# A two-layer attention and convolution trunk: the softmax's division moved into the output gate

## The chip, the cores and the metric

The kernel runs on one core of one Trainium2 chip. The metric is the device time of one execution in microseconds; the time before is the median of three runs, 1473.94 us (1473.72 to 1475.07). The profiled execution is a further one. The core's engines are TensorE (PE, with its weight loads as PEld), VectorE (DVE), ScalarE (ACT), GpSimd (POOL) and SyncE (SP), which issues the DMAs here.

## What is computed

The input x has 256 tokens of 2048 channels, in float32. Two layers follow each other. The first is attention with three groups of 16 heads (windows and dilations 128/1, 512/4, 2048/16), whose three outputs are merged for each head slot by their softmax denominators, and multiplied by a SiLU gate z:

```
proj = rmsnorm(x) @ w_in                       # q, k, v of 3 groups x 16 heads x 128, and z
o_g, lse_g = attention of group g (QK-norm, bias, window)
w = softmax over the groups of lse_g
y = (sum over g of w_g * o_g) * silu(z)        # silu(z) = z * sigmoid(z)
x = x + y @ w_out
```

Merging three softmaxes by their denominators is the same as one softmax over the keys of all three groups, and so the kernel computes it: one set of scores of 512 columns per head and block of 128 tokens. The second layer is a convolution module with gated projections; the change does not touch it.

## The kernel before

All large products are made in three matmuls of rounded parts: an operand is split in a high part `hi` and the remainder `lo`, and hi x hi, lo x hi and hi x lo are summed. `stage` (lines 101 to 111) loads one chunk of weights (128 x 1024), casts it to `hi` on ScalarE (line 109) and subtracts it to `lo` on VectorE or GpSimd (line 110), three chunks ahead of its use. `low_engine` chooses: VectorE for almost all chunks of the input projection, GpSimd for the chunks 3 to 15 of the output projection's 32.

The order of all work is written out by hand. The main loop has one step per chunk, n. A step stages chunk n + 3, issues the matmuls of chunk n, and then runs the functions that `at(n, ...)` entered in a table for this step, in the order in which they were entered. Each engine executes its own instructions in the order of issue. The input projection has 320 chunks: 8 head sets of 40, two heads each; a chunk is 12 matmuls of 512 columns (lines 257 to 259). A chunk of the output projection is 24 matmuls of 256 columns (lines 493 to 496).

While the projection of the next set runs, the heads of one set are worked off in four units (head h and token block b, in the order h0 b0, h0 b1, h1 b0, h1 b1), three steps apart; in the last set, which runs beside the output projection, two steps apart. A unit, whose first step is t, goes through:
- t: `scores` on TensorE (lines 344 to 356);
- t + 1: `softmax` (358 to 371): bias added and the row maximum taken on VectorE, then exp with the row sum on ScalarE (line 371);
- t + 2: `weigh` (373 to 377): the reciprocal of the sum on VectorE (line 375), and the 512 exponentials multiplied by it on GpSimd (line 377);
- t + 3: `turn` (379 to 382): four transpositions on TensorE into a PSUM tile `pt`;
- t + 4: `split` (384 to 391): `pt` into high and low part, on ScalarE and VectorE.

After the second unit of a head come `values` (t + 5, lines 393 to 412), the matmuls with v; `gated` (t + 6, 414 to 420), which adds the two halves of their result and multiplies with the gate; and `y_split` (t + 7).

The gate: `z_take` copies z out of PSUM, scaled by the token's norm factor r0; `z_gate` (333 to 339), once for each token block, computes z / (1 + exp(-z)) with an exp on ScalarE and an addition, a reciprocal and a product on VectorE; `z_turn` (431 to 436) transposes the four 128 x 128 blocks of a set in one step, e + 4, where e is the set's last projection step, into one PSUM tile; `z_put` (438 to 440) copies it to SBUF one step later.

PSUM tiles come from rings. The ring `t` has two buffers, which `turn`, the scores of groups 1 and 2 (`sy`), the transpositions of q and k (`psq`) and `z_turn` use in turn; a new tile waits until the one before the last has been read. In the last set `z_turn` takes the ring `o` of the value matmuls.

Of the kernel before, what the change touches and what calls it, by code (L numbers as in the profile page):

```python
# [11 lines left out]
F32 = mybir.dt.float32  # L12
F32R = mybir.dt.float32r
AF = mybir.ActivationFunctionType
ALU = mybir.AluOpType
AX = mybir.AxisListType

P = 128
# [7 lines left out]
NSET = 8  # L26
# [15 lines left out]
def hybrid_kernel(ctx: ExitStack, tc: tile.TileContext, x_perm, x_nat, vecs, rel, onehot, maskrow,  # L42
                  w_in, w_out, v_in, v_out, out):
    nc = tc.nc
    cpool = ctx.enter_context(tc.tile_pool(name="cpool", bufs=1))
# [6 lines left out]
    def bank(tag, name, bufs):  # L52
        return psum.tile([P, 512], F32, tag=tag, name=name, bufs=bufs)
# [4 lines left out]
    def t_tile(name):  # L58
        return bank("t", name, 2)
# [10 lines left out]
    def at(n, fn, *args):  # L70
        steps.setdefault(n, []).append((fn, args))
# [43 lines left out]
    ident = cpool.tile([P, P], F32, name="ident")  # L115
# [5 lines left out]
    def rsqrt_mean(dst, src, count, n):  # L121

        nc.gpsimd.tensor_scalar(dst, src, 1.0 / count, EPS, op0=ALU.mult, op1=ALU.add)  # L123
        nc.gpsimd.tensor_tensor(dst, dst, nhalf[:, :n], op=ALU.pow)  # L124
# [8 lines left out]
    apool = ph1.enter_context(tc.tile_pool(name="apool", bufs=1))  # L133

    r0 = cpool.tile([P, 2], F32, name="r0")
    nr0 = cpool.tile([P, 2], F32, name="nr0")
    gqk = cpool.tile([P, NG], F32, name="gqk")
    ssx = apool.tile([P, S], F32, name="ssx")

# [33 lines left out]
    def token_sums(ps, c0, src):  # L173

        for b in range(2):
            nc.tensor.matmul(ps[:, c0 + b:c0 + b + 1], lhsT=src[:, b * P:(b + 1) * P], rhs=ones, start=True, stop=True)

    def first_norm():
        ps = t_tile("ps_r0")
        token_sums(ps, 0, ssx)  # L180
        st = cpool.tile([P, 2], F32, name="st_r0")
        nc.vector.tensor_copy(st, ps[:, :2])
        rsqrt_mean(r0, st, D, 2)
        nc.gpsimd.tensor_scalar(nr0, r0, -1.0, 0.0, op0=ALU.mult, op1=ALU.add)
        nc.vector.scalar_tensor_tensor(gqk, vec[:, V_QG:V_QG + NG], P ** -0.5, vec[:, V_KG:V_KG + NG],
                                       op0=ALU.mult, op1=ALU.mult)
        nc.sync.dma_start(vec[:, V_HEAD:], vecs[:, V_HEAD:])
# [76 lines left out]
    sets = [Set() for _ in range(NSET)]  # L264
    for hs in range(NSET):
        sets[hs].qk, sets[hs].qn, sets[hs].rq, sets[hs].pq, sets[hs].pp = {}, {}, {}, {}, {}
        sets[hs].hs = hs

    def qk_sums(hs, g):
# [55 lines left out]
    def z_take(hs):  # L325
        acc = acc_a.pop(hs * CG + 4)
        sets[hs].zs = []
        for b in range(2):
            zs = apool.tile([P, S], F32, tag="zs", name=f"zs{hs}_{b}", bufs=2)
            nc.scalar.activation(zs, acc[b][:, 256:512], AF.Copy, scale=r0[:, b:b + 1])  # L330
            sets[hs].zs.append(zs)

    def z_gate(hs, b):
        zs = sets[hs].zs[b]
        e = apool.tile([P, S], F32, tag="e", name=f"e{hs}_{b}", bufs=2)
        nc.scalar.activation(e, zs, AF.Exp, scale=-1.0)
        nc.vector.tensor_scalar(e, e, 1.0, None, op0=ALU.add)
        nc.vector.reciprocal(e, e)
        nc.vector.tensor_tensor(zs, zs, e, op=ALU.mult)

    class Unit:
        pass
# [30 lines left out]
    def weigh(u):  # L373

        nc.vector.reciprocal(u.m[:, 3:4], u.m[:, 2:3])
        pr = u.pr.rearrange("p a b -> p (a b)")
        nc.gpsimd.tensor_scalar(pr, pr, u.m[:, 3:4], 0.0, op0=ALU.mult, op1=ALU.add)  # L377

    def turn(u):
        u.pt = t_tile(f"pt{u.n}").rearrange("p (c q) -> p c q", c=4)  # L380
# [12 lines left out]
    def values(st, h):  # L393

        pp, v01, v2 = st.pp.pop(h), st.v01, st.v2
        st.po = bank("o", f"o{st.hs}_{h}", 1)
        po = st.po
        cs = slice(h * P, (h + 1) * P)
        for i in range(2):
            vh, vl = v01[i]  # L400
            for n, (w, m) in enumerate(((vh, pp[:, i, 1:3, :]), (vh, pp[:, i, 0:4:3, :]), (vl, pp[:, i, 1:3, :]))):

                nc.tensor.matmul(po[:, P:3 * P], lhsT=w[:, cs], rhs=m, start=i == 0 and n == 0, stop=False,
                                 skip_group_check=True)
        for b in range(2):
            q0 = (1 + b) * P
            for i, ((vh, vl), col) in enumerate(((v01[b], 2 + h), (v2[b], h))):
                cs = slice(col * P, (col + 1) * P)
                nc.tensor.matmul(po[:, 2 * b * P:2 * (b + 1) * P], lhsT=vh[:, cs], rhs=pp[:, 2 + i, 2 * b:2 * b + 2, :],
                                 start=False, stop=False, skip_group_check=True)  # L410
                nc.tensor.matmul(po[:, q0:q0 + P], lhsT=vl[:, cs], rhs=pp[:, 2 + i, 1 + b, :],
                                 start=False, stop=i == 1, skip_group_check=True)

    def gated(st, h):
        po = st.po.rearrange("p (c q) -> p c q", c=4)
        xs = apool.tile([P, 2, P], F32, tag="xs", name=f"xs{st.hs}_{h}", bufs=1)
        st.y = apool.tile([P, 2, P], F32, tag="y", name=f"y{st.hs}_{h}", bufs=2)
        nc.scalar.copy(xs, po[:, 0:4:3, :])
        nc.vector.tensor_tensor(st.y, po[:, 1:3, :], xs, op=ALU.add)
        nc.vector.tensor_tensor(st.y, st.y, st.gz[:, h, :, :], op=ALU.mult)  # L420

    def y_split(st, h):

# [4 lines left out]
        nc.scalar.copy(hi, src)  # L428
        nc.vector.tensor_tensor(lo, src, hi.bitcast(F32), op=ALU.subtract)

    def z_turn(hs):
        ps = bank("o", f"pz{hs}", 1) if hs == NSET - 1 else t_tile(f"pz{hs}")
        sets[hs].pz = ps.rearrange("p (h b q) -> p h b q", h=2, b=2)
        for h in range(2):
            for b in range(2):
                nc.tensor.transpose(sets[hs].pz[:, h, b, :], sets[hs].zs[b][:, h * P:(h + 1) * P], ident)

    def z_put(hs):
        sets[hs].gz = apool.tile([P, 2, 2, P], F32, tag="gz", name=f"gz{hs}", bufs=1)
        nc.scalar.copy(sets[hs].gz, sets[hs].pz)  # L440

    for hs in range(NSET):
        n0 = hs * CG * 8
        last = hs == NSET - 1
        for h in range(2):
            at(n0 + 34 + 2 * h, load_bias, 2 * hs + h)
        for g in range(NG):
            e = n0 + g * 8 + 7
            if e == 7:
                at(e + 1, first_norm)  # L450
                at(e + 2, qk_sums, hs, g)
            else:
                at(e + 1, qk_sums, hs, g)
            at(e + 3, qk_norm, hs, g)
            late = 2 * (hs > 0 and g == 0)
            at(e + late + 4, qk_turn, hs, g, 0)
            at(e + late + 5, qk_split, hs, g, 0)
            at(e + 3 * late // 2 + 5, qk_turn, hs, g, 1)
            at(e + 3 * late // 2 + 6, qk_split, hs, g, 1)
        at(n0 + 32, v_split, hs, 0, 512)  # L460
        e = n0 + 39
        at(e + 1 - last, v_split, hs, 1, 256)
        at(e + 1 - last, z_take, hs)
        at(e + 2 + last, z_gate, hs, 0)
        at(e + 3 + 2 * last, z_gate, hs, 1)
        for i in range(4):
            u = Unit()
            u.set, u.h, u.b, u.head, u.n = sets[hs], i // 2, i % 2, 2 * hs + i // 2, f"{hs}_{i}"
            t = e + 1 + 2 * i if last else e + 3 + 3 * i
            for dt, fn in ((0, scores), (1, softmax), (2, weigh), (3, turn), (4, split)):  # L470
                at(t + dt, fn, u)
            if u.b == 1:
                at(t + 5, values, sets[hs], u.h)
                at(t + 6, gated, sets[hs], u.h)
                at(t + 7, y_split, sets[hs], u.h)
        at(e + 4 + 2 * last, z_turn, hs)
        at(e + 5 + 2 * last, z_put, hs)


    oacc = {}  # L480
# [32 lines left out]
    f = Set()  # L513
# [39 lines left out]
    for ct in range(KT):  # L553
# [4 lines left out]
        else:  # L558
            e = N_A + KT + 2 * (ct - 8) + 1
# [214 lines left out]
    for i, un in enumerate(units):  # L774
        e = N_WO + 2 * i + 1
# [9 lines left out]
    for i, un in enumerate(units):  # L785
        e = N_WO + 2 * i + 1
# [127 lines left out]
```

## Time and profile before

| | |
|---|---|
| median of three runs | 1473.94 us (1473.72 to 1475.07) |
| the profiled execution, its own time | 1472.46 us |
| its span, first to last instruction | 1470.7 us |
| granted TensorE clock | 1.0 of full speed throughout |
| busy: TensorE / VectorE / ScalarE / GpSimd | 98% / 67% / 49% / 34% |

The page and the answers of the trace are read like this: times are microseconds from the start of the span unless marked ns. A line as `L382 PE MATMUL pt<-ident,pr` is an instruction of line 382, on TensorE, that writes tile pt from ident and pr; `x4` means four that follow each other, merged. `[1.26 <-POOL pr L377]` means that the engine stood idle for 1.26 us before it, until GpSimd's instruction of line 377 that writes pr had ended. Matmuls overlap, and their ends are modelled, so starts are compared with starts.

### The profile page before, as it was taken

What the parts mean: (1) busy time and instruction counts of PE and PEld (TensorE: products, weight loads), DVE (VectorE), ACT (ScalarE), POOL (GpSimd) and SP (SyncE); (2) the same over time, 40 slices, a digit from 0 to 9 for tenths busy, and PEclk for the clock granted to TensorE, in tenths of its full rate; (3) what the DMA queues carried; (4) which work ended last, traced back from release to release, by engine and by line L of the source; (5) the groups of instructions that cost most, each with busy time, mean ns of one, the idle gap of its engine ahead of it and who ended that gap; (6) DMA issues with size and microseconds to landing.
All of it is one profiled execution on the core that took longest, in us unless ns stands there. A gap on an engine that the chain in (4) does not pass through costs nothing.

```text
span 1470.7 us, 22547 instructions
## 1 busy us (share of the span) xinstructions
PE 1448.6 (98%) x8556; PEld 1277.8 (87%) x8556; DVE 988.7 (67%) x1542; ACT 721.6 (49%) x1011; POOL 493.2 (34%) x394
## 2 busy tenths in 40 slices
PE   8999999999999999999999999999999999999999
PEld 6778888888788888888878888889999999999999
DVE  8656765775675676577567567655658989998621
ACT  5444554454454455445445445544544545455732
POOL 7210220210030022021003002207316979998544
PEclk9999999999999999999999999999999999999999
DMA  7458457457456645745745664566465655555544
GB/s 254 156 185 261 153 188 215 147 170 223 162 160 194 198 154 184 217 150 167 224 159 166 190 201 149 186 170 228 158 201 166 201 180 172 184 190 175 185 161 140
DMA packets 108124, 269.20 MB, mean 183 GB/s; under 512 B 42352, under 2 KB 44656, under 8 KB 108016
## 3 DMA queue, kind: packets, MB, share of 16 engines
q1 hardware_dynamic: 108016, 267.76, 57.6%
q8 instruction: 67, 1.10, 0.3%
q14 instruction: 41, 0.34, 0.1%
HBM read 265.36 MB, written 2.36 MB: 182 GB/s over the span
## 4 chain that ended last, share of the span: by engine, by line
PE 93%; DVE 2%; POOL 2%; ACT 1%; DMA 1%; issue 1%; SPq 0%; ACTq 0%; POOLq 0%; DVEq 0%
PE acc L257 19%; PE acc L259 19%; PE acc L258 18%; PE b L508 6%; PE b L509 6%; PE b L510 6%; PE psq L294 1%; POOL pr L377 1%; ACT hi L109 1%; DMA raw<-w_in 1%; PE vo L510 1%; PE vo L509 1%; PE vo L508 1%; PE vow L496 1%; PE vow L495 1%; PE vow L493 1%
## 5 line engine op out<-in xcount | busy, mean ns | idle before, releaser
L109 ACT CAST hi<-raw 128x1024 fp32r<-128x1024 f32 (+1 forms) x481 | 497.4, 1045 | 297.5 <-PE acc L258 165.3
L110 DVE TENSOR_TENSOR lo<-raw,hi 128x1024 fp32r<-128x1024 f32 (+1 forms) x360 | 444.3, 1238 | 275.6 <-ACT hi L109 267.6
L257 PE MATMUL acc<-hi,xh 128*128 128x512 f32 x1280 | 509.6, 398 | 0.8 <-ACT xh L154 0.8
L259 PE MATMUL acc<-lo,xh 128*128 128x512 f32 x1280 | 501.9, 392 | 3.5 <-DVE lo L110 3.5
L258 PE MATMUL acc<-hi,xl 128*128 128x512 f32 x1280 | 499.7, 390 | 0.4 <-DVE xl L155 0.4
L110 POOL TENSOR_TENSOR lo<-raw,hi 128x1024 fp32r<-128x1024 f32 x121 | 292.8, 2440 | 112.5 <-ACT hi L109 94.6
L259 PEld LDWEIGHTS acc<-lo,xh 128*128 128x128 f32 x1280 | 240.9, 188 | 58.2 <-DVE lo L110 5.7
L257 PEld LDWEIGHTS acc<-hi,xh 128*128 128x128 f32 x1280 | 241.0, 188 | 49.7 <-issue 2.1
L258 PEld LDWEIGHTS acc<-hi,xl 128*128 128x128 f32 x1280 | 241.4, 189 | 48.2 <-DVE xl L155 0.9
L377 POOL TENSOR_SCALAR pr<-pr,m 128x512 f32<-128x512 f32 x32 | 48.7, 1521 | 549.3 <-ACT hi L109 388.0
L508 PE MATMUL b<-hh,hi 128*128 128x256 f32 x768 | 217.8, 284 | 0.0
L509 PE MATMUL b<-hl,hi 128*128 128x256 f32 x768 | 217.3, 283 | 0.0
L510 PE MATMUL b<-hh,lo 128*128 128x256 f32 x768 | 217.3, 283 | 0.0
L655 DVE SCALAR_TENSOR_TENSOR c<-u,vec,c 128x256 f32<-128x256 f32 x464 | 187.5, 482 | 3.5 <-ACT c L651 3.5
L509 PEld LDWEIGHTS b<-hl,hi 128*128 128x128 f32 x768 | 147.4, 192 | 0.0
L508 PEld LDWEIGHTS b<-hh,hi 128*128 128x128 f32 x768 | 147.4, 192 | 0.0
L510 PEld LDWEIGHTS b<-hh,lo 128*128 128x128 f32 x768 | 147.4, 192 | 0.0
L123 POOL TENSOR_SCALAR rq<-ss 128x4 f32<-128x4 f32 x48 | 10.8, 226 | 223.5 <-DVE ss L276 220.7
L371 ACT ACTIVATE pr<-sc,m 128x512 f32<-128x512 f32 x32 | 23.2, 725 | 116.6 <-DVE m L369 116.6
L305 ACT CAST qk<-psq 128x256 fp32r<-128x256 f32 x48 | 17.9, 372 | 76.7 <-PE psq L294 76.7
L307 DVE TENSOR_TENSOR qk<-psq,qk 128x256 fp32r<-128x256 f32 x48 | 20.3, 423 | 49.2 <-ACT qk L306 49.1
L124 POOL TENSOR_TENSOR rq<-rq,nhalf 128x4 f32<-128x4 f32 x48 | 48.4, 1008 | 4.0
(171 smaller groups left out, 1728.6 us busy)
## 6 DMA issues: line engine op xcount, KB each, us to landing
raw<-w_in SPq DMA_DIRECT2D x319, 512.0 KB, 4.2
raw<-v_in SPq DMA_DIRECT2D x96, 512.0 KB, 3.4
raw<-w_out SPq DMA_DIRECT2D x32, 512.0 KB, 3.4
raw<-v_out SPq DMA_DIRECT2D x32, 512.0 KB, 3.9
bt<-btab SPq DMA_DIRECT2D x64, 128.0 KB, 5.2
x<-x_nat SPq DMA_DIRECT2D x4, 512.0 KB, 6.6
out_t<-ob SPq DMA_DIRECT2D x16, 128.0 KB, 1.8
xr<-x_perm SPq DMA_DIRECT2D x7, 256.0 KB, 6.6
```

The source lines that it names most:

```text
L109: nc.scalar.copy(hi[:, sl], raw[:, sl])
L110: low_engine(n).tensor_tensor(lo[:, sl], raw[:, sl], hi[:, sl].bitcast(F32), op=ALU.subtract)
L124: nc.gpsimd.tensor_tensor(dst, dst, nhalf[:, :n], op=ALU.pow)
L257: nc.tensor.matmul(acc[b], lhsT=xh[:, k, sl], rhs=wh, start=k == 0, stop=False)
L258: nc.tensor.matmul(acc[b], lhsT=xl[:, k, sl], rhs=wh, start=False, stop=False)
L259: nc.tensor.matmul(acc[b], lhsT=xh[:, k, sl], rhs=wl, start=False, stop=k == KT - 1)
L371: nc.scalar.activation(u.pr.rearrange("p a b -> p (a b)"), sc, AF.Exp, bias=u.m[:, 1:2], accum_out=u.m[:, 2:3])
L377: nc.gpsimd.tensor_scalar(pr, pr, u.m[:, 3:4], 0.0, op0=ALU.mult, op1=ALU.add)
L508: nc.tensor.matmul(acc, lhsT=wh, rhs=mh[:, k, :], start=k == 0, stop=False)
L509: nc.tensor.matmul(acc, lhsT=wh, rhs=ml[:, k, :], start=False, stop=False)
L510: nc.tensor.matmul(acc, lhsT=wl, rhs=mh[:, k, :], start=False, stop=k == KT - 1)
L655: nc.vector.scalar_tensor_tensor(c[t % 2], u[:, t:t + S], vec[:, cw + t:cw + t + 1], c[t % 2], op0=ALU.mult, op1=ALU.add)
```

## The change

Five things change in the attention layer. The exponentials are no longer multiplied by the reciprocal of their sum; the gate's row, which belongs to the same token, is multiplied by it instead, on VectorE, 128 columns per unit. The gate is computed as 0.5 z (tanh(0.5 z) + 1): r0h holds half of r0, and one VectorE operation replaces three. The gate's transposition and copy are made for each head by itself, after its second unit, in place of once for the set before the units. In `values`, two matmuls of 256 columns with the same v become one of 512, for the high and the low parts of both token blocks together; where the low parts' product is added changes from the middle to the outer columns of the result, which `gated` adds anyway. In the last set the first head's `gated` and `y_split` come one step later, and the gate's PSUM tile comes from ring `t`.

```diff
@@ -133,7 +133,7 @@
     apool = ph1.enter_context(tc.tile_pool(name="apool", bufs=1))
 
     r0 = cpool.tile([P, 2], F32, name="r0")
-    nr0 = cpool.tile([P, 2], F32, name="nr0")
+    r0h = cpool.tile([P, 2], F32, name="r0h")
     gqk = cpool.tile([P, NG], F32, name="gqk")
     ssx = apool.tile([P, S], F32, name="ssx")
 
@@ -181,7 +181,7 @@
         st = cpool.tile([P, 2], F32, name="st_r0")
         nc.vector.tensor_copy(st, ps[:, :2])
         rsqrt_mean(r0, st, D, 2)
-        nc.gpsimd.tensor_scalar(nr0, r0, -1.0, 0.0, op0=ALU.mult, op1=ALU.add)
+        nc.gpsimd.tensor_scalar(r0h, r0, 0.5, 0.0, op0=ALU.mult, op1=ALU.add)
         nc.vector.scalar_tensor_tensor(gqk, vec[:, V_QG:V_QG + NG], P ** -0.5, vec[:, V_KG:V_KG + NG],
                                        op0=ALU.mult, op1=ALU.mult)
         nc.sync.dma_start(vec[:, V_HEAD:], vecs[:, V_HEAD:])
@@ -264,6 +264,7 @@
     sets = [Set() for _ in range(NSET)]
     for hs in range(NSET):
         sets[hs].qk, sets[hs].qn, sets[hs].rq, sets[hs].pq, sets[hs].pp = {}, {}, {}, {}, {}
+        sets[hs].pz, sets[hs].gz = {}, {}
         sets[hs].hs = hs
 
     def qk_sums(hs, g):
@@ -327,16 +328,15 @@
         sets[hs].zs = []
         for b in range(2):
             zs = apool.tile([P, S], F32, tag="zs", name=f"zs{hs}_{b}", bufs=2)
-            nc.scalar.activation(zs, acc[b][:, 256:512], AF.Copy, scale=r0[:, b:b + 1])
+            nc.scalar.activation(zs, acc[b][:, 256:512], AF.Copy, scale=r0h[:, b:b + 1])
             sets[hs].zs.append(zs)
 
     def z_gate(hs, b):
+
         zs = sets[hs].zs[b]
         e = apool.tile([P, S], F32, tag="e", name=f"e{hs}_{b}", bufs=2)
-        nc.scalar.activation(e, zs, AF.Exp, scale=-1.0)
-        nc.vector.tensor_scalar(e, e, 1.0, None, op0=ALU.add)
-        nc.vector.reciprocal(e, e)
-        nc.vector.tensor_tensor(zs, zs, e, op=ALU.mult)
+        nc.scalar.activation(e, zs, AF.Tanh)
+        nc.vector.scalar_tensor_tensor(zs, e, 1.0, zs, op0=ALU.add, op1=ALU.mult)
 
     class Unit:
         pass
@@ -373,8 +373,8 @@
     def weigh(u):
 
         nc.vector.reciprocal(u.m[:, 3:4], u.m[:, 2:3])
-        pr = u.pr.rearrange("p a b -> p (a b)")
-        nc.gpsimd.tensor_scalar(pr, pr, u.m[:, 3:4], 0.0, op0=ALU.mult, op1=ALU.add)
+        zs = u.set.zs[u.b][:, u.h * P:(u.h + 1) * P]
+        nc.vector.tensor_scalar(zs, zs, u.m[:, 3:4], None, op0=ALU.mult)
 
     def turn(u):
         u.pt = t_tile(f"pt{u.n}").rearrange("p (c q) -> p c q", c=4)
@@ -398,10 +398,10 @@
         cs = slice(h * P, (h + 1) * P)
         for i in range(2):
             vh, vl = v01[i]
-            for n, (w, m) in enumerate(((vh, pp[:, i, 1:3, :]), (vh, pp[:, i, 0:4:3, :]), (vl, pp[:, i, 1:3, :]))):
-
-                nc.tensor.matmul(po[:, P:3 * P], lhsT=w[:, cs], rhs=m, start=i == 0 and n == 0, stop=False,
-                                 skip_group_check=True)
+
+            nc.tensor.matmul(po, lhsT=vh[:, cs], rhs=pp[:, i, :, :], start=i == 0, stop=False, skip_group_check=True)
+            nc.tensor.matmul(po[:, P:3 * P], lhsT=vl[:, cs], rhs=pp[:, i, 1:3, :], start=False, stop=False,
+                             skip_group_check=True)
         for b in range(2):
             q0 = (1 + b) * P
             for i, ((vh, vl), col) in enumerate(((v01[b], 2 + h), (v2[b], h))):
@@ -417,7 +417,7 @@
         st.y = apool.tile([P, 2, P], F32, tag="y", name=f"y{st.hs}_{h}", bufs=2)
         nc.scalar.copy(xs, po[:, 0:4:3, :])
         nc.vector.tensor_tensor(st.y, po[:, 1:3, :], xs, op=ALU.add)
-        nc.vector.tensor_tensor(st.y, st.y, st.gz[:, h, :, :], op=ALU.mult)
+        nc.vector.tensor_tensor(st.y, st.y, st.gz.pop(h), op=ALU.mult)
 
     def y_split(st, h):
 
@@ -428,16 +428,14 @@
         nc.scalar.copy(hi, src)
         nc.vector.tensor_tensor(lo, src, hi.bitcast(F32), op=ALU.subtract)
 
-    def z_turn(hs):
-        ps = bank("o", f"pz{hs}", 1) if hs == NSET - 1 else t_tile(f"pz{hs}")
-        sets[hs].pz = ps.rearrange("p (h b q) -> p h b q", h=2, b=2)
-        for h in range(2):
-            for b in range(2):
-                nc.tensor.transpose(sets[hs].pz[:, h, b, :], sets[hs].zs[b][:, h * P:(h + 1) * P], ident)
-
-    def z_put(hs):
-        sets[hs].gz = apool.tile([P, 2, 2, P], F32, tag="gz", name=f"gz{hs}", bufs=1)
-        nc.scalar.copy(sets[hs].gz, sets[hs].pz)
+    def z_turn(st, h):
+        st.pz[h] = t_tile(f"pz{st.hs}_{h}")
+        for b in range(2):
+            nc.tensor.transpose(st.pz[h][:, b * P:(b + 1) * P], st.zs[b][:, h * P:(h + 1) * P], ident)
+
+    def z_put(st, h):
+        st.gz[h] = apool.tile([P, 2, P], F32, tag="gz", name=f"gz{st.hs}_{h}", bufs=2)
+        nc.scalar.copy(st.gz[h].rearrange("p b q -> p (b q)"), st.pz.pop(h)[:, :2 * P])
 
     for hs in range(NSET):
         n0 = hs * CG * 8
@@ -471,10 +469,12 @@
                 at(t + dt, fn, u)
             if u.b == 1:
                 at(t + 5, values, sets[hs], u.h)
-                at(t + 6, gated, sets[hs], u.h)
-                at(t + 7, y_split, sets[hs], u.h)
-        at(e + 4 + 2 * last, z_turn, hs)
-        at(e + 5 + 2 * last, z_put, hs)
+                if last and u.h == 0:
+                    t += 2
+                at(t + 4, z_turn, sets[hs], u.h)
+                at(t + 5, z_put, sets[hs], u.h)
+                at(t + 6 - (last and u.h == 0), gated, sets[hs], u.h)
+                at(t + 7 - (last and u.h == 0), y_split, sets[hs], u.h)
 
 
     oacc = {}
```

## Rows read from the trace of the kernel before

**Rows 1.** The page's part 1: engine, busy us, share of the span, instructions.
```profile
PE 1448.6 (98%) x8556; PEld 1277.8 (87%) x8556; DVE 988.7 (67%) x1542; ACT 721.6 (49%) x1011; POOL 493.2 (34%) x394
```

**Rows 2.** The page's part 4: the chain that ended last, by engine.
```profile
PE 93%; DVE 2%; POOL 2%; ACT 1%; DMA 1%; issue 1%; SPq 0%; ACTq 0%; POOLq 0%; DVEq 0%
```

**Rows 3.** TensorE's waits: for whom, us in total, times, longest us.
```profile
PE pt L382 <- POOL pr L377: 11.0, 8, 2.0
```

**Rows 4.** Timeline of ScalarE, VectorE, GpSimd, first set: start us, us, instruction [idle before].
```profile
147.59 0.72 ACT L371 ACTIVATE pr<-sc,m 128x512 f32<-128x512 f32 x1 [6.52 <-DVE m L369]
...
150.52 0.15 DVE L375 RECIPROCAL m<-m 128x1 f32<-128x1 f32 x1
...
150.85 2.80 POOL L377 TENSOR_SCALAR pr<-pr,m 128x512 f32<-128x512 f32 x1 [53.96 <-ACT hi L109]
```

**Rows 5.** Timeline of TensorE at the first set's first unit.
```profile
152.05 0.39 PE L259 MATMUL acc<-lo,xh 128*128 128x512 f32 x1
153.70 0.66 PE L382 MATMUL pt<-ident,pr 128*128 128x128 f32 x4 [1.26 <-POOL pr L377]
```

**Rows 6.** Timeline of TensorE at the first set's second unit.
```profile
162.97 0.40 PE L259 MATMUL acc<-lo,xh 128*128 128x512 f32 x1
163.21 0.60 PE L382 MATMUL pt<-ident,pr 128*128 128x128 f32 x4
...
164.42 0.44 PE L257 MATMUL acc<-hi,xh 128*128 128x512 f32 x1
```

**Rows 7.** Timeline of TensorE in the last set: second unit, fourth unit.
```profile
1011.24 0.28 PE L496 MATMUL wow<-yh,lo 128*128 128x256 f32 x1
1013.54 0.66 PE L382 MATMUL pt<-ident,pr 128*128 128x128 f32 x4 [2.02 <-POOL pr L377]
...
1028.68 0.28 PE L496 MATMUL wow<-yh,lo 128*128 128x256 f32 x1
1028.81 0.60 PE L382 MATMUL pt<-ident,pr 128*128 128x128 f32 x4
1029.16 0.36 PE L493 MATMUL wow<-yh,hi 128*128 128x256 f32 x1
```

**Rows 8.** The chain in order of time: start us, us on the chain, what.
```profile
139.52 0.23 PE acc L257
...
142.24 0.23 PE acc L257
...
146.51 0.44 PE pz L436 x4
...
170.11 0.71 PE o L403 x6
...
1021.18 0.70 PE o L403 x6
```

**Rows 9.** Line 337 alone: ns shortest/median/longest, first and last start us.
```profile
L337 DVE TENSOR_SCALAR e<-e x16: 286/289/2389, 138.5 to 1007.5; 128x256 f32<-128x256 f32 x16
```

**Rows 10.** Instructions grouped by line: busy us, mean ns | idle us before, releaser.
```profile
L377 POOL TENSOR_SCALAR pr<-pr,m 128x512 f32<-128x512 f32 x32 | 48.7, 1521 | 549.3 <-ACT hi L109 388.0 <-DVE m L375 117.7 <-ACT sq L274 43.6
...
L338 DVE RECIPROCAL e<-e 128x256 f32<-128x256 f32 x16 | 28.1, 1753 | 0.5
...
L339 DVE TENSOR_TENSOR zs<-zs,e 128x256 f32<-128x256 f32 x16 | 6.8, 425 | 0.6
...
L615 ACT ACT_TABLE_LOAD x1 | 1.3, 1283 | 0.0
```

**Rows 11.** Timeline of VectorE at the first set's second unit.
```profile
164.46 0.69 DVE L391 TENSOR_TENSOR pp<-pt,pp 128x512 fp32r<-128x512 f32 x1 [0.35 <-ACT pp L390]
```

**Rows 12.** Timeline of VectorE and GpSimd in the last set.
```profile
998.75 2.39 DVE L337 TENSOR_SCALAR e<-e 128x256 f32<-128x256 f32 x1 [2.20 <-ACT e L336]
...
1016.88 0.69 DVE L391 TENSOR_TENSOR pp<-pt,pp 128x512 fp32r<-128x512 f32 x1 [2.36 <-ACT pp L390]
...
993.85 7.14 POOL L110 TENSOR_TENSOR lo<-raw,hi 128x1024 fp32r<-128x1024 f32 x3 [42.10 <-ACT hi L109]
```

## The prediction

> **What bounds the kernel now.** First the busy shares, then the chain of waits that ended last, then TensorE's own waits, and only then single stretches. TensorE is busy for 98% of the span [rows 1] and holds 93% of the chain [rows 2], so a microsecond is gained only where TensorE stands still or where its own instructions become cheaper. Its waits are few: eight for the product of line 377, 11.0 us in all, the longest 2.0 us [rows 3]. That is one for each of the eight head sets, in front of the first (in the last set the second) transposition of the probabilities at line 382. The other waits in that view belong to the start of the kernel or to single places, and the change touches none of them.
>
> One such wait, in the first set: ScalarE has the exponentials at 148.31 (147.59 + 0.72). VectorE, which executes in order, comes to the reciprocal of their sum only at 150.52. GpSimd then multiplies the 512 columns until 153.65 [rows 4]. TensorE started its last matmul at 152.05 and the transposition only at 153.70 [rows 5], 1.65 us from start to start. In the next unit, which doesn't wait, the same two starts lie 0.24 us apart (162.97 and 163.21) [rows 6].
>
> **The change part by part.**
>
> *Line 377 leaves the path.* The transposition afterwards needs only the exponentials. Against the 152.28 at which TensorE would take it up (152.05 and 0.23 of a matmul), they are 4.0 us early [rows 4, 5], so nothing takes the place of the wait there. A set's gain: 1.65 - 0.24 = 1.41 us of start to start, and 0.06 us by which the group of four transpositions is longer after a wait (0.66 against 0.60) [rows 5, 6]; 1.47 us. The wait view gives the seven that are not the longest (11.0 - 2.0) / 7 = 1.29 us each [rows 3], as this one has 1.26 [rows 5], so I take seven times 1.47 = 10.3 us. In the last set the two starts lie 2.30 us apart (1011.24 and 1013.54) where 0.13 us is the distance without a wait (1028.68 and 1028.81) [rows 7]: 2.17 + 0.06 = 2.2 us. Together 12.5 us, a little over the 11.0 us of the wait view, which counts from a modelled end of the matmul before. The ends for this term are 11.0 and 12.5; I take 12.5, since starts are measured and ends are modelled.
>
> *The value matmuls.* Per head six of 256 columns become two of 512 and two of 256. Six of 256 took 0.71 us, 0.118 each; 512 columns cost 0.227 each (12 matmuls between the starts 139.52 and 142.24) [rows 8]. Per head 4 x 0.118 - 2 x 0.227 = 0.02 us, with 16 heads 0.3 us. The same columns pass, so more than that is not to be had; at the least it is nothing.
>
> *The gate's transpositions.* Four per set (0.44 us [rows 8]) become two and two, so their own time stays. In seven sets one pair goes into a step of its own, as the four did, and the other to a step that already has the transpositions of q and k; the number of interruptions stays. In the last set two interruptions replace one that hung on line 382's. One whole four-transposition insertion cost 0.35 us there (1028.81 to 1029.16) [rows 7], so two more cost between nothing and 0.7 us; I take 0.2, since the transpositions themselves are not new.
>
> *The gate by tanh.* On VectorE three operations per token block go: the addition (0.29 us median [rows 9]), the reciprocal (1.753 us) and the product (0.425 us) [rows 10]. One two-tensor operation of the product's size comes, for which I take the product's price. That is 16 x 2.04 = 33 us less. The tanh replaces an exp of the same size. All of it lies beside TensorE's work, so I count nothing. What it does do is bring the exponentials forward: that ACT instruction had waited 6.52 us for VectorE [rows 4], which was behind the gate's reciprocals.
>
> *The scaling of the gate.* 32 times VectorE takes one operation of 128 columns, between the 0.155 us of a one-column reciprocal [rows 4] and the 0.286 us of the 256-column addition [rows 9]; with 0.22 that is 7 us, so VectorE is lighter by some 26 us in all. Hidden by TensorE's chunk of 2.72 us. GpSimd loses 32 operations of 1.5 us (48.7 us) [rows 10], all of them off its own limit. Their cover matters in one place only: behind the scaling on VectorE stands the next unit's softmax, and ScalarE's exp waits for that.
>
> *The gate's copy.* Eight copies of 512 columns become 16 of 256. An ACT instruction over 512 columns took 0.72 us [rows 4], so eight more of half that size bring ScalarE less than 5.8 us of work, spread over eight sets and hidden. No DMA moves, and nothing is moved past a DMA.
>
> *What is late next.* The PSUM ring "t" has two buffers. The first head's gate now takes the buffer of the second unit's transposed probabilities, which split empties in that very step. In the trace split's subtraction ends at 165.15 (164.46 + 0.69) [rows 11], while TensorE, which starts the chunk after those scores at 164.42 [rows 6], ends it 2.72 us later, at 167.1: 2.0 us to spare. The second head's pair is followed at once by q and k's, which needs the fourth unit's buffer, in the same position. Between nothing and a stall, I take nothing, because VectorE only gets lighter ahead of it.
>
> Sum: -12.5 - 0.3 + 0.2 = -12.6 us. The profiled execution took 1472.46 us (span 1470.7), so 1459.9 for it. The median of the timed runs lies 1.5 us above it; the change has no reason to alter that, so 1473.94 - 12.6 = 1461.3 us.
>
> **A rule against it.** In the last set GpSimd is busy with the low parts of the output weights, and VectorE's addition for the gate there took 2.39 us, from 998.75 to 1001.14, ending with GpSimd's run of three that began at 993.85 and lasted 7.14 us [rows 12]; elsewhere it took 0.29 us [rows 9]. [...] Four scalings and two products of the new kernel fall into this stretch. By the rows, six times up to 2.1 us on VectorE stand against two such waits and the 2 x 1.75 us of reciprocals that go: about 5 us more on VectorE at worst, over a stretch of some 40 us. I count it in the first rival.
>
> **The rivals.**
> 1. *The last set keeps its stall, at another place.* VectorE, held up by GpSimd, is late with the split of the second unit. That split ended at 1017.57 (1016.88 + 0.69) [rows 12], and the value matmuls followed at 1021.18 [rows 8]; without the 2.2 us stall TensorE is there at 1019.0, so a split 1.4 us later makes it wait. For it: the worst case above. Against: the reciprocals' 3.5 us leave that very queue, and four of GpSimd's multiplications leave the other. It gives back up to 2.2 us: 1463.5.
> 2. *Tanh costs a table load beside each exp.* The trace shows three loads of 1.28 us in the whole kernel [rows 10], none for tanh. Two switches in each of seven sets and four in the last would be 18 x 1.28 = 23 us on ScalarE. The exponentials have 4.0 us to spare in an ordinary set, so most stays hidden: 1461.3 to 1463.5, or half the gain lost (1467.6) if casts of the weights are pushed late as well. [...]
> 3. *Slower: the PSUM ring.* If the split comes more than 2.0 us later against TensorE, every gate transposition waits, with the whole in-order matmul stream behind it: two waits in each of eight sets. From 0.8 us per wait (2.8 us of delay) the 12.6 us are gone; at 1.8 us each, 28.8 us, it is 1490.1. For it: the reuse within one step is new. Against: 2.0 us of room and a lighter VectorE.
> 4. *No gain*: the wait moves whole to another operand of the same transposition: about 1473.6.
>
> **How the numbers follow.** What a measurement here can tell from no change is about 0.2%, 2.9 us. My forecast has 0.72, with its own range of 1459.4 to 1462.8 (the 11.0 end of the main term, and 1.5 us between executions). Rival 1 has 0.13 (1463.5), the dear form of rival 2 0.07 (1467.6), no gain 0.03, slower 0.05. So faster 0.92, same 0.03, slower 0.05. The range of 1459.0 to 1466.0 holds the forecast and rival 1, and leaves out the rest.
>
> **What would show it.** Right: the row of waits of line 382 for GpSimd is gone with no other wait of TensorE above 0.5 us in the eight sets; starts of consecutive sets some 1.5 us closer than before; value groups of four matmuls at 0.69 us; still three table loads; TensorE's busy time lower by under 1 us. Wrong: gate transpositions or value matmuls that wait for VectorE or ScalarE, more table loads, or the first transposition of a set waiting for the exponentials.

## The result, and the profile after

The changed kernel takes 1458.54 us (median of four runs, 1458.15 to 1458.98), the kernel before 1473.83 us in the same comparison: a ratio of 0.9897, with a 95% interval of 0.9881 to 0.9913. That is 15.3 us less, where the prediction had 12.6 us and a range down to 1459.0: the sign was right, the size too small by 2.7 us, and the time lies 0.5 us below the range. The profiled execution took 1458.98 us, its span 1457.2 us.

The page of the changed kernel, part 1 and the engines' shares of part 4 (for [rows 1] and [rows 2]):

```profile
PE 1444.3 (99%) x8524; PEld 1275.6 (88%) x8524; DVE 973.8 (67%) x1542; ACT 723.0 (50%) x1019; POOL 449.7 (31%) x362
...
PE 96%; DVE 2%; DMA 1%; issue 1%; SPq 0%; ACT 0%; POOL 0%; POOLq 0%; DVEq 0%; ACTq 0%
```

GpSimd and ScalarE hold 0% of the chain now. TensorE's waits, in the columns of [rows 3]; the row of line 382 is gone, and all that is left belongs to the first 100 us or to a single place of the second layer:

```profile
PE acc L259 <- DVE lo L110: 4.6, 7, 0.7
PE ps_warm L169 <- POOL ident masks.py:199: 1.4, 1, 1.4
PE acc L258 <- DVE xl L155: 0.9, 1, 0.9
PE acc L257 <- ACT xh L154: 0.9, 1, 0.9
PE psq L295 <- DVE row L219: 0.8, 1, 0.8
PE ps_rn L567 <- DVE rn L722: 0.7, 1, 0.7
PE psq L295 <- DVE qn L287: 0.4, 1, 0.4
```

Timeline of the changed kernel in the first set, TensorE, ScalarE and VectorE (for [rows 4] and [rows 5]):

```profile
143.41 0.52 PE L351 MATMUL s<-qk 128*128 128x256 f32 x3
...
152.20 0.39 PE L259 MATMUL acc<-lo,xh 128*128 128x512 f32 x1
152.43 0.60 PE L382 MATMUL pt<-ident,pr 128*128 128x128 f32 x4
...
146.01 0.72 ACT L371 ACTIVATE pr<-sc,m 128x512 f32<-128x512 f32 x1 [4.30 <-DVE m L369]
...
141.36 0.42 DVE L339 SCALAR_TENSOR_TENSOR zs<-e,zs 128x256 f32<-128x256 f32 x1
...
148.95 0.15 DVE L375 RECIPROCAL m<-m 128x1 f32<-128x1 f32 x1
149.14 0.29 DVE L377 TENSOR_SCALAR zs<-zs,m 128x128 f32<-128x128 f32 x1
```

From TensorE's last matmul to the transposition it is 0.23 us, as between units that never waited [rows 6]. Two things differ upstream. The exponentials come at 146.01, where they came at 147.59 before [rows 4], although the unit's scores start 0.65 us later in this execution (143.41, against 142.76 in the timeline of before). And the reciprocal of their sum stands at 148.95 in place of 150.52: even GpSimd's 1.5 us of multiplication after it would now have been in time.

The distance between sets is read from the first transposition of probabilities in the first set and in the seventh, on the chain in order of time. Before, and then after:

```profile
153.70 0.66 PE pt L382 x4
...
887.88 0.66 PE pt L382 x4
```

```profile
152.59 0.44 PE pt L382 x4
...
876.72 0.44 PE pt L382 x4
```

That is (887.88 - 153.70) / 6 = 122.36 us before and (876.72 - 152.59) / 6 = 120.69 us after; 1.67 us per set, where the prediction's terms come to some 1.5. All distances below are found in this way.

### The profile page after: what moved, and what is told of

The parts are those of the page before. It is cut to its first block, busy times and chain, and to the rows that moved or that the text cites. A ratio compares the mean times of both kernels' runs of the same rounds, so it can differ in the third digit from the quotient of the medians.

```text
span 1457.2 us, 22415 instructions
## 1 busy us (share of the span) xinstructions
PE 1444.3 (99%) x8524; PEld 1275.6 (88%) x8524; DVE 973.8 (67%) x1542; ACT 723.0 (50%) x1019; POOL 449.7 (31%) x362
## 4 chain that ended last, share of the span: by engine, by line
PE 96%; DVE 2%; DMA 1%; issue 1%; SPq 0%; ACT 0%; POOL 0%; POOLq 0%; DVEq 0%; ACTq 0%
PE acc L257 20%; PE acc L259 19%; PE acc L258 19%; PE b L508 6%; PE b L509 6%; PE b L510 6%; PE psq L295 1%; PE wow L493 1%; PE vo L510 1%; PE wo L510 1%; PE wo L509 1%; PE vo L509 1%; PE vow L496 1%; PE vow L495 1%; PE vow L493 1%; PE vo L508 1%
## 5 line engine op out<-in xcount | busy, mean ns | idle before, releaser
L390 ACT CAST pp<-pt 128x512 fp32r<-128x512 f32 x32 | 18.8, 587 | 44.1 <-PE pt L382 44.1
```

## The experiments

Each was timed beside the kernel before; the two further profiles of before were single runs. `before` is 1474.2 us beside the first four rows of the table, 1473.0 beside the next two and 1473.6 beside the last two.

| kernel | median, us (lowest to highest, runs) | ratio to before, interval | distance of sets, us | wait left in the sets |
|---|---|---|---|---|
| changed, again | 1458.46 (1457.66 to 1458.62, 4) | 0.9889, 0.9873 to 0.9906 | 120.69 | none |
| division alone | 1462.78 (1461.01 to 1463.18, 4) | 0.9918, 0.9903 to 0.9933 | 120.76 | 2.1, last set |
| tanh alone | 1459.94 (1459.78 to 1460.25, 4) | 0.9901, 0.9887 to 0.9916 | 120.87 | none |
| changed, narrow values | 1458.87 (1458.38 to 1458.96, 4) | 0.9893, 0.9878 to 0.9908 | 120.76 | none |
| changed, product on GpSimd | 1458.58 (1458.19 to 1458.88, 4) | 0.9897, 0.9881 to 0.9914 | 120.69 | none |
| changed, merged turn | 1457.62 (1457.36 to 1457.89, 4) | 0.9891, 0.9877 to 0.9906 | 120.60 | none |
| tanh in the last set alone | 1470.32 (1469.99 to 1471.89, 11) | 0.9978, 0.9969 to 0.9987 | 122.35 | 9.0, seven sets |
| tanh in seven sets | 1463.33 (1461.96 to 1463.71, 5) | 0.9928, 0.9914 to 0.9942 | 120.87 | 2.0, last set |

**The changed kernel again.** No edit.

> The changed kernel, unaltered, timed again beside the kernel before. The two profiles differ by 13.5 us, the two medians by 15.3 us. Theory A (the profiled execution of before fell low among its own runs and that of the changed kernel high, so part of the surplus over the predicted 12.6 us is spread between executions): the difference of medians comes out at 13 to 14 us, ratio about 0.9908. Theory B (the whole 15.3 us is in the kernel, and the profile hides some of it): 15 us or more, ratio 0.990 or below.

1458.46 against 1474.21 us: 15.7 us, inside theory B's terms. The surplus is no accident of one comparison. It does not show in the two profiles (1472.46 and 1458.98 us, 13.5 us apart). So the further profiles of before went after executions of the kernel before that the first profile had not caught.

**The division alone.** The gate stays exp, sum and reciprocal, and the value matmuls narrow:

```diff
-        nc.gpsimd.tensor_scalar(pr, pr, u.m[:, 3:4], 0.0, op0=ALU.mult, op1=ALU.add)
+        zs = u.set.zs[u.b][:, u.h * P:(u.h + 1) * P]
+        nc.vector.tensor_scalar(zs, zs, u.m[:, 3:4], None, op0=ALU.mult)
...
+    def z_turn(st, h):   # per head, with z_put, as in the change
```

> Only the division moves into the gate, with the transposition per head that it needs; the gate by exp, sum and reciprocal and the narrow value matmuls stay. Theory A (line 377 was the last link before the first transposition of a set, and the exponentials have 4 us to spare): all eight waits are gone and the gain is that of the whole change but for 0.3 to 0.5 us: 13 us, about 1459.5 to 1460.5 us. Rival (the wait came from VectorE's reciprocals in the gate, which hold up the softmax): the waits stay in part, now for ScalarE's exponentials, and the gain is under 7 us.

The seven ordinary waits went, as theory A said; the last set kept one. Gain 11.4 us, between the two. What the wait is, from the timeline of its last set, VectorE, GpSimd, TensorE (lines are shifted by two):

```profile
996.70 2.27 DVE L339 TENSOR_SCALAR e<-e 128x256 f32<-128x256 f32 x1 [2.14 <-ACT e L338]
999.01 1.75 DVE L340 RECIPROCAL e<-e 128x256 f32<-128x256 f32 x1
1000.79 0.69 DVE L341 TENSOR_TENSOR zs<-zs,e 128x256 f32<-128x256 f32 x1
1001.40 0.68 DVE L393 TENSOR_TENSOR pp<-pt,pp 128x512 fp32r<-128x512 f32 x1
...
996.42 4.78 POOL L110 TENSOR_TENSOR lo<-raw,hi 128x1024 fp32r<-128x1024 f32 x2 [4.38 <-PE wow L499]
...
999.74 0.28 PE L499 MATMUL wow<-yh,lo 128*128 128x256 f32 x1
1002.14 0.88 PE L384 MATMUL pt<-ident,pr 128*128 128x128 f32 x4 [2.12 <-DVE pp L393]
```

The second unit's transposition waits for a buffer of the ring t, which the first unit's split has not emptied; that split stands on VectorE behind the gate's addition, which took 2.27 us beside GpSimd's low parts (0.289 in the median before [rows 9]), and behind the gate's reciprocal of 1.75 us. This is the prediction's third rival (the ring) brought about by its first (VectorE late in the last set); it came only where the reciprocals stayed.

The wait is not all that this kernel loses there. In the profiled execution (1462.56 us) TensorE's granted clock lies at 0.50 behind it; busy time by stretch, columns PE, PEld, DVE, ACT, POOL with instructions, then the clock, DMA share and GB/s:

```profile
1003.00:1004.00 1.00, 1.00 (x7) 1.00 (x6) 0.93 (x3) 0.00 (x0) 0.00 (x0) 0.50 0.88 336
1004.00:1005.00 1.00, 1.00 (x7) 1.00 (x6) 0.31 (x1) 0.59 (x1) 0.00 (x0) 0.50 0.10 33
```

What that costs is measured below, on the kernel before; one of the four runs here, at 1461.01 us, lies 1.5 us and more below the others.

**Tanh alone.**

```diff
-        nc.scalar.activation(e, zs, AF.Exp, scale=-1.0)
-        nc.vector.tensor_scalar(e, e, 1.0, None, op0=ALU.add)
-        nc.vector.reciprocal(e, e)
-        nc.vector.tensor_tensor(zs, zs, e, op=ALU.mult)
+        nc.scalar.activation(e, zs, AF.Tanh)
+        nc.vector.scalar_tensor_tensor(zs, e, 1.0, zs, op0=ALU.add, op1=ALU.mult)
```

> Only the gate by tanh; the multiplication on GpSimd, the one transposition per set and the narrow value matmuls stay. Theory A as predicted (the multiplication is the cause, the tanh lies beside TensorE's work and counts nothing): the waits for line 377 stay near 11 us and the time near 1473. Rival (the gate's reciprocals were what made the whole chain late; without them the exponentials are some 2 us or more earlier, and the 1.3 us wait of seven sets is covered): the seven ordinary waits go, the last set's shrinks to about 0.4 us, and the gain is 11 to 12 us, about 1462. Then either half of the change would have been enough.

The rival holds, and more than holds: all eight waits are gone, the last set's too, for a gain of 14.3 us. GpSimd's product of the first set, its timeline in this kernel:

```profile
148.41 1.76 POOL L375 TENSOR_SCALAR pr<-pr,m 128x512 f32<-128x512 f32 x1 [51.51 <-ACT hi L109]
```

It ends at 150.17, where it ended at 153.65 before [rows 4], and TensorE comes for it at 152.08. Of the 3.5 us, 2.4 are its earlier start and 1.0 is its own time, 1.76 in place of 2.80 us. The same multiplication is on the path or off it according to what stands on VectorE ahead of the softmax.

**The changed kernel with narrow values.**

```diff
-            nc.tensor.matmul(po, lhsT=vh[:, cs], rhs=pp[:, i, :, :], start=i == 0, stop=False, skip_group_check=True)
+            for n, (w, m) in enumerate(((vh, pp[:, i, 1:3, :]), (vh, pp[:, i, 0:4:3, :]), (vl, pp[:, i, 1:3, :]))):
...
```

> The changed kernel with the value matmuls back to six of 256 columns. Theory A (a 512-column matmul saves 0.01 us over two of 256): 0.3 to 0.5 us slower than the changed kernel, value groups of 0.71 in place of 0.70 us on the chain. Rival (the surplus of 0.2 us per set over the predicted gain comes from the value matmuls): 1.2 us or more slower, with a longer stretch after the value groups.

0.3 to 0.4 us slower than the changed kernel's two medians and 0.07 us more per set: theory A. The rival is out.

**Two more profiles of the kernel before.** No edit.

> The kernel before, unaltered, for a second profile. Its timed runs spread over 3.3 us (1472.3 to 1475.6), those of the changed kernel over 1.0 us, and the first profile was of a run near the low end. Theory A (the length of the eight waits differs between executions, since they end with GpSimd's line 377, whose duration depends on what VectorE does at that moment): a slower execution shows longer waits at line 382, some 1.5 us each in place of 1.3, the same start and the same second half. Theory B (the start of the kernel, where the first loads land, spreads): the distance between sets stays 122.35 us and the first transposition comes later.

> The same once more: a third profile of the kernel before, at another of its times. Theory A: time and total of the waits at line 382 go together from profile to profile. Theory B: time and the moment of the first set's first transposition go together.

The first took 1472.81 us, with the same distance of sets and the same waits (11.5 us in all); its start was 0.3 us later. The second, the third profile of before, took 1473.96 us and fits neither theory: its waits are 11.2 us in all, its first transposition comes at 153.60, 0.1 us earlier than in the first profile, and its sets are 122.37 us apart. Its extra 1.5 us lie in the last set. Busy time by stretch there, in the same columns as above; the first profile of before, and then this one:

```profile
1011.00:1014.00 3.00, 0.98 (x9) 0.78 (x8) 2.90 (x8) 0.00 (x0) 1.22 (x2) 1.00 0.38 153
1014.00:1017.00 3.00, 3.00 (x28) 3.00 (x27) 0.64 (x2) 2.39 (x5) 2.35 (x2) 1.00 0.10 19
```

```profile
1011.00:1014.00 3.00, 0.96 (x7) 0.76 (x6) 2.90 (x8) 0.00 (x0) 1.30 (x2) 0.93 0.36 139
1014.00:1017.00 3.00, 3.00 (x16) 3.00 (x15) 0.64 (x2) 2.47 (x5) 2.33 (x2) 0.50 0.12 27
```

Behind the same wait of 2.0 us TensorE's granted clock is 0.50 in place of 1.00, and it does 16 instructions in 3 us where it did 28. From the transposition to the next scores it takes 5.36 us (1013.46 to 1018.82) in place of 3.80 (1013.54 [rows 7] to 1017.34): 1.56 us. TensorE's timelines, the third profile and then the first:

```profile
1013.46 1.06 PE L382 MATMUL pt<-ident,pr 128*128 128x128 f32 x4 [2.04 <-POOL pr L377]
...
1018.82 0.51 PE L351 MATMUL s<-qk 128*128 128x256 f32 x3
```

```profile
1017.34 0.51 PE L351 MATMUL s<-qk 128*128 128x256 f32 x3
```

**The changed kernel, product on GpSimd.**

```diff
-        zs = u.set.zs[u.b][:, u.h * P:(u.h + 1) * P]
-        nc.vector.tensor_scalar(zs, zs, u.m[:, 3:4], None, op0=ALU.mult)
+        pr = u.pr.rearrange("p a b -> p (a b)")
+        nc.gpsimd.tensor_scalar(pr, pr, u.m[:, 3:4], 0.0, op0=ALU.mult, op1=ALU.add)
```

> The changed kernel with one thing undone: GpSimd multiplies the exponentials again and the gate is not scaled; tanh, transposition per head and wide value matmuls stay. Theory A (after the tanh the product is early enough: it ended 2.1 us ahead of its use where only the tanh was changed): no wait at line 382, time within 1 us of the changed kernel, 1458 to 1460, so the division's move is worth nothing by itself once the tanh is there. Rival (the prediction's reading, that line 377 is the link that costs): the waits come back, 1469 or more. It also shows what shortens a set by 0.13 us between tanh alone (120.87) and the changed kernel with narrow values (120.74): if the per-head transposition does, the distance is 120.7 here, if the division's move does, 120.8.

Theory A: 1458.58 us and no wait. With the tanh in place, the division's move is worth nothing that can be measured. And the distance is 120.69 us, so what shortens a set from 120.87 to 120.76 us beside the value matmuls comes with the transposition per head, not with the division.

**Tanh in the last set alone, and in the other seven alone.**

```diff
+        if hs == NSET - 1:          # the other kernel: hs < NSET - 1
+            nc.scalar.activation(e, zs, AF.Tanh)
+            nc.vector.scalar_tensor_tensor(zs, e, 1.0, zs, op0=ALU.add, op1=ALU.mult)
+        else:
             nc.scalar.activation(e, zs, AF.Exp, scale=-1.0)
...
```

> Tanh in the last set alone; the other seven sets keep exp, sum and reciprocal, everything else as before. Theory A (the last set's wait of 2 us lets TensorE's clock fall in some executions, as the third profile of before showed, 1.5 us lost over it; this is what lifts before's median over its profile and spreads its runs): the wait there goes, and with it the spread: runs within 1 us of each other, seven waits of 1.3 us left, about 1470.0; 3 to 4.5 us below the median of before, where the wait itself is worth only 2.3. Rival (the spread comes from the start of the kernel or from elsewhere): the gain is 2.3 us, the runs spread over 3 us as before.

> Tanh in the first seven sets; the last keeps exp, sum and reciprocal. Theory A: the seven waits of 1.3 us go (7 x 1.48 = 10.4 us), the last set's of 2 us stays and with it the fall of the clock in some executions: fast ones at 1462.0, slow ones at 1463.5 or above, a spread of 2 to 3 us, and a low granted clock behind that wait whenever the profiled run is a slow one. Rival (the spread comes from the start or from the seven waits): runs within 1 us of each other, at 1462.

With the last set's wait gone, nine of eleven runs lie between 1469.99 and 1470.46 us (the others at 1471.0 and 1471.9), while the 15 runs of before beside them spread from 1471.9 to 1476.8. With that wait kept and the other seven gone, the five runs form two groups, 1461.96 and 1462.04, and 1463.33 to 1463.71. The profiled run is of the second, and the same columns show the low clock behind its last set's wait:

```profile
1002.00:1004.00 2.00, 0.71 (x6) 0.71 (x7) 1.93 (x6) 0.00 (x0) 1.46 (x2) 1.00 0.01 2
1004.00:1006.00 2.00, 2.00 (x14) 2.00 (x13) 0.27 (x1) 1.64 (x3) 1.58 (x1) 0.66 0.05 8
1006.00:1008.00 2.00, 2.00 (x11) 2.00 (x11) 0.76 (x2) 2.00 (x4) 1.76 (x1) 0.50 0.60 213
```

Both theories A hold in the main: two of the eleven runs stay out of the narrow group, and the five runs spread over 1.8 us where 2 to 3 were expected. What the wait itself costs is read from the seventh set's first transposition to the last set's fourth, on the chain, before (where the seventh set's is the 887.88 above) and with tanh in the last set alone:

```profile
1028.97 0.44 PE pt L382 x4
```

```profile
888.12 0.66 PE pt L386 x4
...
1026.77 0.44 PE pt L386 x4
```

That is 141.09 and 138.65 us: 2.4 us for the wait, and in a part of the executions 1.5 us more.

The timed runs of before agree with it as far as they can. Each run's mean granted clock is on record: the seven runs of before with a mean of 1.000 took 1471.9 to 1473.0 us, and 18 of the other 22 took 1473.4 or more. A lower mean alone does not tell where the clock fell. In the second profile of before (0.998) the stretch from 10 to 20 us has 0.83, and those behind the wait have 1.00, and of the five runs with tanh in seven sets the two quick ones have 0.998 and 0.997, the three others 0.998 and 0.999. For runs that were not profiled, the fall behind the wait is inferred from their times.

**The changed kernel, merged turn.** The gate's pair goes into the step that transposes probabilities, in seven sets:

```diff
-        st.pz[h] = t_tile(f"pz{st.hs}_{h}")
+        st.pz[h] = t_tile(f"pz{st.hs}_{h}") if st.hs == NSET - 1 else bank("o", f"pz{st.hs}_{h}", 1)
...
-                at(t + 4, z_turn, sets[hs], u.h)
-                at(t + 5, z_put, sets[hs], u.h)
+                at(t + 3 + last, z_turn, sets[hs], u.h)
+                at(t + 4 + last, z_put, sets[hs], u.h)
```

> The changed kernel with the gate's transpositions of seven sets moved one step ahead, into the steps that already transpose probabilities, and into the ring of the value matmuls in place of the ring t; the last set as it is. Theory A (an interruption of the stream of large matmuls costs some 0.05 us beside its own instructions): one interruption less per set, distance between sets 120.64 in place of 120.69 us, 0.3 to 0.4 us in all, about 1458.1. Rival (the ring t was holding something, or the gate's scaling comes too late for the earlier step): waits of TensorE at the gate's transposition, slower than 1459.

1457.62 us, 0.09 us less per set, no new wait. All its runs lie below the changed kernel's median. The intervals of the two ratios overlap, so the time alone leaves it open; the set distances, which repeat to 0.01 us, show the gain. The edit moves the pair to another step and to another ring at once; which of the two brings it was not separated.

## Why the prediction was wrong, point by point

**The step that failed: the base.** "The median of the timed runs lies 1.5 us above it; the change has no reason to alter that." It had one. The 1.5 us were no fixed offset between a profile and a timed run. In some executions TensorE's granted clock falls to 0.50 behind the last set's 2 us wait, the very wait that the change removes, and the third profile, at 1473.96 us, shows one of them at the median itself. The first profile (1472.46 us) was one in which it stayed at 1.00, so nothing in it showed a price beyond the wait's own length. In the changed kernel the profiled run is 0.4 us above the median. This accounts for 1.5 + 0.4 = 1.9 of the 2.8 us between the predicted 1461.3 and 1458.54 us. That the clock falls, and that this cost 1.56 us in the third profile, is shown; how often it falls is inferred from the times of the runs. The other 0.9 us lie mainly with the gate's transpositions, below.

**Line 377 off the path: 12.5 us predicted.** The size was right: 122.36 - 120.87 = 1.49 us per set with tanh alone, where the waits are gone and nothing else is changed on TensorE (1.47 predicted), and 2.4 us in the last set (2.2 predicted). The transpositions of the first and the seventh set in that kernel:

```profile
152.24 0.44 PE pt L380 x4
...
877.48 0.44 PE pt L380 x4
```

The cause was half seen. The wait had two sufficient remedies, and the prediction named one.

**The gate by tanh: "All of it lies beside TensorE's work, so I count nothing."** Wrong as a price for the edit: it brings 14.3 us by itself. The prediction had the pieces, the 6.52 us for which the exp waited for VectorE and the reciprocals ahead of it, and named them as a help to the exponentials, without following them through the reciprocal of the sum and GpSimd's product to the transposition. The sum came out all the same, because the two edits remove the same wait and it can be counted once only.

**The value matmuls, 0.3 us predicted:** 0.07 us per set and 0.3 to 0.4 us in time. Right.

**The gate's transpositions, a cost of 0.2 us predicted:** a gain instead. Their own time stayed and no wait came, but between tanh alone and the changed kernel with narrow values a set is 0.12 us shorter, some 0.8 us in seven sets. In the traces of the first set, five of the six stretches that begin with transpositions of q and k are each 0.02 to 0.03 us shorter. Why the matmuls behind such an interruption take less was not tried and stays open.

**Scaling, copies, tables.** The scaling took 0.287 us (median), just above the 0.286 us allowed for it at most and above the 0.22 taken, and hidden. The trace has three table loads of 1.28 us, at lines 171, 615 and 768, as before, and none at the tanh: the rival of the reloads is out.

**The first rival's mechanism is there, but has no price here.** Lines 377 and 339 of the changed kernel, shortest, median and longest in ns:

```profile
L377 DVE TENSOR_SCALAR zs<-zs,m x32: 285/287/2232, 149.1 to 1012.6; 128x128 f32<-128x128 f32 x32
...
L339 DVE SCALAR_TENSOR_TENSOR zs<-e,zs x16: 416/419/2581, 139.9 to 996.5; 128x256 f32<-128x256 f32 x16
```

In the last set they take up to 2.2 and 2.6 us beside GpSimd's low parts: the longest of each start at 990.33 and 987.64, within a run of four low parts from 982.79 to 992.47. No wait of TensorE follows; with the reciprocals still in that queue one of 2.1 us does, as the division alone showed.

**The signs of being right.** The waits, the distance of sets, the three table loads and the value groups (0.69 us, from 168.87 to 169.56 in the first set) came as written. TensorE's busy time did not: it fell by 4.3 us, from 1448.6 to 1444.3, where under 1 us was expected. Tanh alone, with its matmuls unaltered, already has 1446.0 us, so a good half of the fall goes with the waits.

The account: 7 x 1.49 = 10.4 us for the seven waits, 2.4 for the last, 0.8 for the shorter stretches and 0.4 for the values make 14.0 us. Less the 0.65 us by which the changed kernel's profiled execution was late at its first scores, that is 13.4, against 13.5 us between the two profiled spans. With up to 1.5 us for the clock the 14.0 become up to 15.5, against a measured 15.3 (12.8 to 17.5 by the interval, which is too wide to tell such terms apart).

## What to carry to other kernels

When an engine waits, follow the chain back past the last link, through the queues of the engines that fed it (in the first set of before, VectorE stood idle until 149.38 ahead of a low part, while the sum had been ready since 148.41 and its reciprocal came behind that low part, at 150.52 [rows 4]): each link that can be shortened by more than the wait is a remedy of its own, and edits that remove the same wait are counted once. If the timed runs of a kernel spread more than those of its relatives, or its profile lies at the low end of them, look for what happens in some executions only before carrying the distance over as an offset. A wait of the matmul engine can cost more than its length: the one of 2.0 us here cost 2.4 us, and 1.5 us more where the granted clock behind it was 0.50.

## What the runs showed of the hardware that was not expected

- After one wait of 2.0 or 2.1 us in a stream that was otherwise dense, TensorE's granted clock was 0.50 for some 3 us in three of the five profiles with such a wait, and 1.00 in two; on the kernel before both were seen, and it cost 1.5 us where it fell. Behind the seven waits of 1.3 us the first profile of before shows 1.00 each time. Four of 15 runs of before lie 1 to 3 us above even that (1474.9 to 1476.8 us, at mean clocks of 0.997 to 0.999); none of them was profiled, and their cause is open.
- VectorE's scaling of 128 columns by a value per token took 0.287 us, its addition of a constant over 256 columns 0.289 [rows 9]: between these two, half the columns saved nothing.
- GpSimd's product of 512 columns took 0.70, 1.50 or 2.8 us in one kernel, with one at 1.16. The 2.8 us ones stand in front of the seven ordinary waits [rows 4]; as an estimate, at 1.50 us the first would have ended at 152.35, 0.07 us after TensorE would have come for it. VectorE ran its low parts of line 110 for 2.3 us beside the 2.8 us ones, for 0.9 us beside those of 1.50, and not beside the others.
